# The fourteenth image's store cut into 112 partitions and four pieces of four

## The chip, the cores and the metric

The kernel runs on one core of a Trainium2 chip. Its time is the device time of one execution in microseconds (us), and the median over several executions is what is compared. One execution was also taken with the hardware profiler. A core has sixteen DMA engines that carry all loads and stores, and five instruction streams: PE (TensorE), DVE (VectorE), ACT (ScalarE), POOL (GpSimd) and SP (SyncE), the last of which only issues transfers here.

## The reference

The kernel computes a 3 x 3 convolution with dilation 2 and zero padding, over 16 images of 64 channels and 64 x 64 pixels, to 128 output channels, in float32.

```python
batch, c_in, h, w, c_out, k, dilation = 16, 64, 64, 64, 128, 3, 2
...
x_pad = np.pad(x, ((0, 0), (0, 0), (pad, pad), (pad, pad)), mode='constant')
...
output[b, co] += weight[co, ci, kh, kw] * x_pad[b, ci, kh*dilation:kh*dilation+h, kw*dilation:kw*dilation+w]
```

The output of one image is 128 channels of 64 x 64 float32 values, 16 KB a channel and 2 MB in all; sixteen images are 33.55 MB. The input is half of that.

## The kernel before

Two images are worked on at a time, since one has 64 input channels and there are 128 partitions. The loop over `pb` (line 174 on) runs over the eight pairs; `hb` is 0 or 1 for the two images of a pair, so image number `2 * pb + hb`, counted from 0. The fourteenth image is number 13: `pb` is 6 (`NP - 2`) and `hb` is 1.

A pair's input is loaded by POOL's queue (`load`, line 72), which turns float32 into float16 on the way. POOL then adds pairs of rows (`prepare`, line 127); with these sums the kernel gets two output rows out of fewer products (`phase`, line 171, on PE). ACT copies the part that two outputs share out of PSUM (line 192), and DVE adds it to each of the two other parts and writes the finished rows into an output tile `o` (line 198). An output tile has one channel in each of the 128 partitions, with 16 KB in each.

The stores stand at the end of the loop over `u`, the four quarters of an image. All of them are issued by SP, in program order, on one queue (line 209). The first and the last pair leave in two halves of 1 MB for each image (8 KB in each partition), and all others in one transfer of 2 MB (16 KB in each partition). So there are 20 stores in all: 4 + 12 + 4. The fourteenth image's is the last of the 2 MB ones; after it come the four 1 MB halves of images 14 and 15.

The kernel's own order is kept (`manual_schedule`), and the framework adds the semaphores. Each transfer reports to a semaphore on landing; SP's transfers take eight such semaphores in turn, the load of the weights (line 63) being the first. Ahead of a transfer that takes a semaphore again, the framework puts an instruction on SP that waits until the earlier transfer with that semaphore, eight before it, has landed. At the end of the program (line 240) SP waits for all transfers.

Of the kernel before, what the change touches and what calls it, by code (L numbers as in the profile page):

```python
# [10 lines left out]
def kernel(  # L11
# [7 lines left out]
    nc = tc.nc  # L19
# [7 lines left out]
    P = 128  # L27
    f32 = mybir.dt.float32
    f16 = mybir.dt.float16
    NP = B // 2  # L30
# [38 lines left out]
    def load(pb, cuts):  # L69
        x16[pb] = x16pool.tile([P, H, W], f16, tag="x16", name=f"x16_{pb}")  # L70
        for lo, hi in zip(cuts, cuts[1:]):
            nc.gpsimd.dma_start(out=x16[pb][:, lo:hi], in_=x_pair[pb, :, lo:hi])  # L72
# [21 lines left out]
    for name, a in (("w21", 2), ("w01", 0)):  # L94
        for u in range(2):
            nc.vector.tensor_sub(  # L96
                out=w16[:, SLOT[name] * KW : (SLOT[name] + 1) * KW, u, :],
# [5 lines left out]
    for n, name in enumerate(("w1", "w21", "w0", "w01", "w2")):  # L103
        ps = cpool.tile([P, NB], f32, tag="ps", name=f"wt{n}")
        k0 = SLOT[name] * KW
        for j in range(KW):
            nc.tensor.matmul(  # L107
                out=ps[:, j * CO : (j + 1) * CO],
# [12 lines left out]
    def prepare(pb, lo, hi):  # L121
        if pb not in s16:
            s16[pb] = sumpool.tile([P, 2 * NQ, W], f16, tag="s16", name=f"s16_{pb}")
        src = x16[pb].rearrange("p (q e r) w -> p q e (r w)", e=2, r=2)
        dst = s16[pb].rearrange("p (q r) w -> p q (r w)", r=2)
        q0, q1 = lo // 4, hi // 4
        nc.gpsimd.tensor_add(  # L127
            out=dst[:, q0:q1], in0=src[:, q0:q1, 0, :], in1=src[:, q0:q1, 1, :]
        )
# [37 lines left out]
    def phase(pb, u, terms):  # L167
        ps = [cpool.tile([CO, NB], f32, tag="ps", name=f"ps{hb}") for hb in range(2)]
        for pair in zip(*(conv(pb, hb, ps[hb], u, terms) for hb in range(2))):
            for m in pair:  # L170
                nc.tensor.matmul(**m)  # L171
        return ps

    for pb in range(NP):
        o = [
            opool.tile([P, H, W], f32, tag="o", name=f"o{pb}_{hb}") for hb in range(2)
        ]
        ov = [t.rearrange("p (q e r) w -> p q e (r w)", e=2, r=2) for t in o]
        for u in range(NU):

            if u == 1 and AHEAD <= pb + 2 < NP:
                load(pb + 2, [0, H])
            if pb + 1 < NP:
                if u == 1:
                    prepare(pb + 1, 0, 36)
                elif u == 2:
                    prepare(pb + 1, 36, H)

            s32 = []
            for hb, ps in enumerate(phase(pb, u, [("w1", 2, 0)])):  # L190
                s = spool.tile([P, NB], f32, tag="s32", name=f"s32_{hb}")
                nc.scalar.copy(out=s, in_=ps)  # L192
                s32.append(s)
            for e, terms in enumerate(
                ([("w21", 1, 0), ("w0", 1, -1)], [("w01", 0, 0), ("w2", 0, 1)])
            ):
                for hb, ps in enumerate(phase(pb, u, terms)):
                    nc.vector.tensor_add(  # L198
                        out=ov[hb][:, u * UQ : (u + 1) * UQ, e, :],
                        in0=ps.rearrange("p (q c) -> p q c", c=QW),  # L200
                        in1=s32[hb].rearrange("p (q c) -> p q c", c=QW),
                    )


            step = NU // 2 if pb in (0, NP - 1) else NU
            if (u + 1) % step == 0:
                fl = slice((u + 1 - step) * 4 * UQ, (u + 1) * 4 * UQ)
                for hb in range(2):
                    nc.sync.dma_start(out=out[2 * pb + hb, :, fl], in_=o[hb][:, fl])


# [33 lines left out]
```

## Time and profile before

| What | Value |
|---|---|
| Median of 3 executions | 128.56 us (127.48 to 129.21) |
| The profiled execution's own time | 128.92 us |
| Its span, first to last instruction | 127.1 us |
| PE busy | 105.3 us (83%) |
| DVE busy | 83.2 us (65%) |
| ACT, POOL busy | 38.8 us, 39.6 us |
| Stores, queue 1 | 3024 packets, 33.85 MB with the weights, 63.1% of 16 engines |
| Loads, queue 0 | 1296 packets, 8.39 MB as written, 32.5% of 16 engines |
| Mean rate of DMA over the span | 333 GB/s |

The difference between the profiled time and its span, 1.8 us, lies outside of the first and the last instruction. A packet here is one row of a transfer: the part that lies in one partition, 16 KB or 8 KB in the stores. Besides these there are 4-byte packets, with which each engine reports that its part of a transfer is done; sixteen such reports make a landing. The trace has the time of each packet and of each report, though not the number of the engine.

### The profile page before, as it was taken

The page shows a single profiled execution, that of the slowest core. Times are in us where ns is not written, and L with a number is a line of the kernel's source. Part 1 is how long each engine was busy: PE and PEld are TensorE (multiplying, and loading weights), DVE is VectorE, ACT ScalarE, POOL GpSimd, SP SyncE. Part 2 cuts the span into 40 slices and gives each one's busy share as a digit, 9 for nine tenths or more (in the row PEclk, how much of TensorE's full clock was granted, in tenths as well). Part 3 has the DMA queues.
Part 4 walks back from the last instruction along what each step waited for, and adds up shares of the span by engine and source line. Part 5 has one row for each costly group of instructions (what it writes and reads, how often), then busy time and mean ns, then how long its engine had stood idle before and what let it go on. Part 6 is the DMA issues. An engine that isn't in the chain of part 4 may idle for free.

```text
span 127.1 us, 2415 instructions
## 1 busy us (share of the span) xinstructions
PE 105.3 (83%) x981; PEld 53.4 (42%) x981; DVE 83.2 (65%) x136; ACT 38.8 (31%) x69; POOL 39.6 (31%) x33
## 2 busy tenths in 40 slices
PE   6329999999999999999999999999999999900000
PEld 2014455555555555555555555555555555400000
DVE  0540577787778777877777787778777877740000
ACT  4723033333333333333333333333333333300000
POOL 6039798668094019302900390000000000000000
PEclk9975699999999999999999999999999999985555
DMA  4899999999999999999999999999999999999940
GB/s 107 152 206 226 214 214 216 250 294 281 402 302 265 312 317 325 399 376 309 304 389 428 423 423 438 433 423 423 433 428 433 418 428 433 433 399 430 430 204 13
DMA packets 4330, 42.38 MB, mean 333 GB/s; under 512 B 480, under 2 KB 480, under 8 KB 864
## 3 DMA queue, kind: packets, MB, share of 16 engines
q1 hardware_dynamic: 3024, 33.85, 63.1%
q0 software_dynamic: 1296, 8.39, 32.5%
q8 instruction: 7, 0.11, 0.3%
q14 instruction: 3, 0.02, 0.0%
HBM read 17.07 MB, written 33.55 MB: 398 GB/s over the span
## 4 chain that ended last, share of the span: by engine, by line
PE 79%; DMA 6%; POOL 1%; issue 1%; DVE 1%; DVEq 0%; POOLq 0%
PE ps L171 79%; DMA x<-in_x_dram 6%; POOL s L127 1%; DVE o L198 1%; DVEq L240 0%; POOLq L226 0%; DVEq L198 0%
## 5 line engine op out<-in xcount | busy, mean ns | idle before, releaser
L198 DVE TENSOR_TENSOR o<-ps,s 128x512 f32<-128x512 f32 x128 | 79.7, 684 | 25.1 <-PE ps L171 22.6
L171 PE MATMUL ps<-x,w_sb 64*128 64x496 f16 (+3 forms) x768 | 86.0, 370 | 0.0
L171 PEld LDWEIGHTS <-w_sb 64*128 64x128 f16 x960 | 51.9, 95 | 52.2 <-issue 4.9
L192 ACT COPY s<-ps 128x512 f32<-128x512 f32 x64 | 34.4, 589 | 68.2 <-issue 60.8
L127 POOL TENSOR_TENSOR s<-x 128x1152 f16<-128x1152 f16 (+4 forms) x18 | 34.0, 1912 | 35.5 <-PE ps L171 29.2
L171 PE MATMUL ps<-s,w_sb 64*128 64x496 f16 (+1 forms) x192 | 26.4, 379 | 2.7 <-POOL s L127 2.7
L72 POOL DMA_DIRECT2D x<-in_x_dram x9 | 5.1, 570 | 0.8 <-POOLq L226 0.8
L87 PE MATMUL warm<-zero 128*128 128x512 f16 x6 | 2.7, 630 | 1.2 <-DVE zero L81 1.2
L96 DVE TENSOR_TENSOR w<-w 128x192 f16<-128x192 f32 x4 | 1.7, 494 | 2.5 <-DMA w<-in_weight_dram 2.5
L93 ACT CAST w<-w 128x576 f16<-128x576 f32 x2 | 2.3, 1217 | 1.6 <-DMA w<-in_weight_dram 1.6
L107 PE MATMUL wt<-ident,w 128*128 128x128 f16 x15 | 1.0, 220 | 2.1 <-ACT w L93 2.1
L116 DVE CAST w_sb<-wt 128x384 f16<-128x384 f32 x3 | 1.5, 550 | 1.0 <-PE wt L107 1.0
L107 PEld LDWEIGHTS <-w 128*128 128x128 f16 x15 | 0.8, 98 | 3.0 <-ACT w L93 3.0
L87 PEld LDWEIGHTS <-zero 128*128 128x128 f16 x6 | 0.7, 138 | 2.3 <-DVE zero L81 1.2
L93 ACT ACT_TABLE_LOAD x1 | 1.3, 1283 | 0.7 <-PEq L226 0.7
L118 ACT CAST w_sb<-wt 128x384 f16<-128x384 f32 x2 | 0.9, 482 | 0.6 <-PE wt L107 0.6
L81 DVE MEMSET zero<- 128x256 uint32 x1 | 0.3, 272 | 0.9 <-PEq L226 0.9
masks.py:199 POOL TENSOR_SCALAR_AFFINE_SELECT ident<-ident 128x128 f16<-128x128 f16 x1 | 0.3, 292 | 0.1
masks.py:197 POOL MEMSET ident<- 128x128 f16 x1 | 0.2, 231 | 0.0
L226 POOL MEMSET const-float32-0.0<- 128x1 f32 x1 | 0.1, 98 | 0.2 <-issue 0.2
L226 POOL MEMSET const-bfloat16-1.0<- 128x1 bf16 x1 | 0.1, 101 | 0.0
L226 POOL MEMSET const-uint8-127<- 128x1 uint8 x1 | 0.1, 101 | 0.0
(1 smaller groups left out, 0.1 us busy)
## 6 DMA issues: line engine op xcount, KB each, us to landing
out_dram<-o SPq DMA_DIRECT2D x12, 2048.0 KB, 17.9
out_dram<-o SPq DMA_DIRECT2D x8, 1024.0 KB, 14.0
x<-in_x_dram POOLq DMA_DIRECT2D x7, 1024.0 KB, 15.0
x<-in_x_dram POOLq DMA_DIRECT2D x1, 576.0 KB, 7.1
x<-in_x_dram POOLq DMA_DIRECT2D x1, 448.0 KB, 8.5
w<-in_weight_dram SPq DMA_DIRECT2D x1, 288.0 KB, 2.9
```

What stands on the lines that cost most here:

```text
L72: nc.gpsimd.dma_start(out=x16[pb][:, lo:hi], in_=x_pair[pb, :, lo:hi])
L87: nc.tensor.matmul(out=warm, lhsT=zero[:, 0:P], rhs=zero, start=True, stop=True)
L93: nc.scalar.copy(out=w16[:, 0:NK, u, :], in_=w32k)
L96: nc.vector.tensor_sub(out=w16[:, SLOT[name] * KW : (SLOT[name] + 1) * KW, u, :], in0=w32k[:, a * KW : (a + 1) * KW, :], in1=w32k[:, KW : ...
L107: nc.tensor.matmul(out=ps[:, j * CO : (j + 1) * CO], lhsT=w16[:, k0 + j, :, :].rearrange("o t i -> o (t i)"), rhs=ident, start=True, stop= ...
L116: nc.vector.tensor_copy(out=dst, in_=ps[:, 0 : KW * CO])
L118: nc.scalar.copy(out=dst, in_=ps[:, 0 : KW * CO])
L127: nc.gpsimd.tensor_add(out=dst[:, q0:q1], in0=src[:, q0:q1, 0, :], in1=src[:, q0:q1, 1, :])
L171: nc.tensor.matmul(**m)
L192: nc.scalar.copy(out=s, in_=ps)
L198: nc.vector.tensor_add(out=ov[hb][:, u * UQ : (u + 1) * UQ, e, :], in0=ps.rearrange("p (q c) -> p q c", c=QW), in1=s32[hb].rearrange("p (q ...
L226: nc = _bacc.Bacc("TRN2", target_bir_lowering=False, num_devices=1)
```

## The change

One store of the twenty, that of the fourteenth image, becomes five: partitions 0 to 111 in one transfer, and then 112 to 115, 116 to 119, 120 to 123 and 124 to 127, each in one of its own. The same 2 MB go from the same tile to the same place. All other stores are as they were, and so is everything else.

```diff
                 for hb in range(2):
-                    nc.sync.dma_start(out=out[2 * pb + hb, :, fl], in_=o[hb][:, fl])
+
+                    parts = [0, P]
+                    if (pb, hb) == (NP - 2, 1):
+                        parts = [0, *range(P - 16, P + 1, 4)]
+                    for lo, hi in zip(parts, parts[1:]):
+                        nc.sync.dma_start(
+                            out=out[2 * pb + hb, lo:hi, fl], in_=o[hb][lo:hi, fl]
+                        )
```

## The prediction

> **What bounds the kernel now.** I began with the slices of the span. The first three lines below are the PE row, the DMA row and the rate, 3.18 us a slice.
>
> ```profile
> PE   6329999999999999999999999999999999900000
> DMA  4899999999999999999999999999999999999940
> GB/s 107 152 206 226 214 214 216 250 294 281 402 302 265 312 317 325 399 376 309 304 389 428 423 423 438 433 423 423 433 428 433 418 428 433 433 399 430 430 204 13
> ```
>
> PE is done after slice 35, at about 111 us. The DMA engines are full from slice 3 to 38, and once the loads are over (slice 22 on) they stand at 418 to 438 GB/s, a ceiling that nothing crosses for long. The last two slices are the oddity: 204 and 13 GB/s. Next, the chain of work that ended last: its last pieces are DVE's and it stops at 112.77 us, 14 us ahead of the end of the span. What follows is in SP's waits.
>
> ```profile
> 110.89 0.68 DVE o L198
> ...
> 112.17 0.60 DVE o L198
> ```
>
> ```profile
> SPq L240 <- DMA out_dram<-o: 12.0, 5, 2.4
> SPq L209 <- DVE o L198: 4.8, 2, 4.7
> ```
>
> Five waits of some 2.4 us each: SP stands at the program's end and sees the last five stores land one after another. The end is set by landings, not by arithmetic. Then the tail by windows (window, length, five engines' busy time, clock, DMA share, GB/s), and the DMA view of the last stretch, 123.3 to 127 us.
>
> ```profile
> 120.00:121.00 1.00, 0.00 (x0) 0.00 (x0) 0.00 (x0) 0.00 (x0) 0.00 (x0) 0.50 1.01 426
> 121.00:122.00 1.00, 0.00 (x0) 0.00 (x0) 0.00 (x0) 0.00 (x0) 0.00 (x0) 0.50 0.81 344
> 122.50:123.00 0.50, 0.00 (x0) 0.00 (x0) 0.00 (x0) 0.00 (x0) 0.00 (x0) 0.50 0.24 98
> 124.00:125.00 1.00, 0.00 (x0) 0.00 (x0) 0.00 (x0) 0.00 (x0) 0.00 (x0) 0.50 0.06 25
> ```
>
> ```profile
> DMA packets 8, 0.06 MB, mean 15 GB/s; under 512 B 1, under 2 KB 1, under 8 KB 1
> q1 hardware_dynamic: 8, 0.06, 3.7%
> ```
>
> A share of 0.06 is one engine of sixteen. Fifteen engines have finished by 123.3 us; one works on alone at 25 GB/s through seven rows of 8 KB and its report. The trace's reports of the last store come at 121.40 us (first), 123.56 (fifteenth) and 126.07 (sixteenth). So the kernel ends 2.5 us late because of one laggard. Its lag grew through the run (0.36 us at the store that landed at 75.2 us, 2.16 at 106.2, 2.54 at 116.3): its 16 KB rows mostly took 634 to 661 ns where the others' took 611, until PE stopped.
>
> **The change part by part.** One row of 16 KB occupies an engine for 0.607 us (a 611 ns packet, the next one starting 4 ns before its end; 16 x 16,384 B / 0.607 us is 432 GB/s, the ceiling above). A store of 128 rows is 8 rows an engine, 4.86 us.
>
> Removed: the fourteenth image's transfer loses 16 rows. If 112 rows are dealt evenly, each engine has 7, one less: -0.61 us on every engine, the laggard too.
>
> Added: four transfers of four rows. The trace has no transfer of fewer than 128 rows, so this is bounded. Lower end: the rows go to four engines, the same four each time, at full speed and not to the laggard. These four get 7 + 4 = 11 rows, +1.82 us, and end at 123.56 + 1.82 = 125.38 at the latest; the laggard ends at 126.07 - 0.61 = 125.46. Sum: -0.61 us. Upper end: the four rows of a piece leave as through one engine, because they sit on one or share one way out of the memory. A piece then takes 4 x 0.607 = 2.43 us, four take 9.71, and with the 7 rows before them (4.25) that is 13.96 against 4.86, +9.10 us. The engines concerned would have reported between 121.40 and 123.56, so they report between 130.50 and 132.66: +4.43 to +6.59 us on the end, in the middle +5.5. Between the two, I take the upper. The row of the trace that is nearest to a small transfer is the lone stretch above, the only place where fewer than sixteen engines carry rows, and there rows move at 25 GB/s, one after another. The lower end needs three things at once (four engines, no sharing, the laggard not among them); the upper needs one. It is a choice without a direct row for it, and both ends stay.
>
> [...]
>
> The 112 rows: seven rows an engine don't sit as eight did. If two engines share a way for all of it, seven rows cost up to 4.25 us more, if not, nothing. No row shows it; I take nothing in the middle, since the streams at the ceiling lose nothing to each other, and half of it, 2.1 us, for the top of the range.
>
> Instructions on SP: four more issues of 0.33 to 1.02 us (the rows of this line), each with a 0.22 us semaphore wait ahead of it. The five issues begin at 100.42 us and by the dear price end at 100.42 + 5 x 1.24 = 106.6, where the next store is issued at 105.86 now: up to 0.8 us late. Cost nothing, as the engines have rows of the fourteenth image until the first report of it at 111.61. Without that backlog it would be 0.8.
>
> Waits moved: eight semaphores in turn. The small pieces wait for images 6 to 9, all landed by 95.89 us. Images 14 and 15, first halves, now wait for images 10 and 11 (101.04 and 106.20; issued at 105.86 and 106.46), image 14's second half for image 12 (111.36; issued at 112.19): nothing. The last store, issued at 112.79 now, waits for the 112 rows, which land at 116.30 - 0.61 = 115.7. It is issued at 115.9, and its first packet follows 1.0 us (the weights: issue 0.74, packet 1.74) to 3.7 us later (the first store: 19.27, 22.99), at 116.9 to 119.6. The earliest engine wants it at about 118 (it reports the store before at 118.96), the laggard at 123. Early engines may idle up to 1.6 us and would still report by 119.6 + 2.45 + 0.4 = 122.5, under the end; only the program's end is queued behind it on SP. Cost nothing; without the laggard's cover up to 1.6.
>
> Sum against the profiled 128.92 us: -0.61 removed, the rest in the +9.10 on the four engines, less the 2.5 to 4.7 us that they finish early: +5.5, so 134.4 us in such an execution. The median of runs lies 0.36 below it: 134.1.
>
> **The rivals.** *It balances.* The lower end is the truth: the laggard gives up one row, four others take three each, and all end near 125.4. Time 128.56 - 0.61 = 127.95, faster and not slower. For it: the lag is real (2.5 us), and -0.61 and +1.82 meet almost exactly. Against it: the three conditions. It turns into the forecast where a small row takes long enough: slower by 2% (2.57 us) begins when the four engines report at 128.64, 5.08 us or 8.4 rows later than the fifteenth does now, that is when the four small rows take 9.4 row times, 1.43 us each.
>
> *The laggard is among the four,* or rows share in part: 126.07 + 1.82 = 127.89, time 130.4, inside of 2%. For it: nothing tells which engine lags; against: four of sixteen.
>
> *It does less or more than it says.* If a row goes to the engine that carried it in the 128-row store, whichever transfer it is in, loads are as before: 128.56. If 112 rows keep their engines and the laggard loses four, it gains at most 4 x 0.607 = 2.43 us, and the time is 126.1 at best, still under 2%. For these: nothing but the constant order of the reports from store to store.
>
> **How the numbers follow.** Forecast (small pieces go as through one engine) 0.56; it balances 0.22; laggard among them or part sharing 0.14; less or more than it says 0.08. The likeliest gives 134.1; its own range is 128.56 + 4.43 = 133.0 less a us for partly staggered engines, 132.0, to 128.56 + 6.59 + 2.1 = 137.3. For 8 in 10 the whole must hold the balanced case with the scatter of the runs (0.7 us): 127.3 to 137.3. A change of 2% is about what a measurement of this kernel can tell from none. Slower than that: 0.58, the forecast and a tail of part sharing; within: 0.37; faster: 0.05, the best of the third rival with a favourable scatter.
>
> **What would show it.** If right: the windows show a share of about 0.25 or less, near 27 to 110 GB/s, for some 5 us at the end, instead of 0.06 for 2.5; 16 KB packets after about 110 us last 1.2 to 2.4 us instead of 611 ns; the fourteenth image's small issues land 2.4 us apart. If it balances: packets stay at 611 ns, five engines end together near 125.4, and the lone stretch is gone. The last issue near 115.9 us instead of 112.8 would show the semaphore step right. A median under 131.1 us makes the forecast wrong, and packets that stay at 611 ns make its reason wrong.

## The result, and the profile after

The changed kernel took 133.89 us (median of 6, 131.90 to 137.08) against 128.47 us before: a ratio of 1.033, interval 1.027 to 1.040. Repeated on two more occasions beside other kernels it was 1.047 (1.041 to 1.054) and 1.036 (1.031 to 1.042). Ratios leave out executions more than 1.5% above the fastest of their kernel, so that the medians of the changed kernel, which scatters widely, lie further from those before than its ratios say, and of the profiles of such executions (the two halves and the 112 rows alone, further down, among them) only packets, rates and landings are read. The profile shown here is of an execution of the second occasion, at 132.86 us with a span of 131.1.

The slices of the changed kernel (3.28 us each; PE, DMA, rate):

```profile
PE   6339999999999999999999999999999999000000
DMA  4899999999999999999999999999999999999720
GB/s 105 151 222 211 227 212 197 285 280 307 410 312 285 330 307 320 350 315 320 355 425 440 420 425 440 420 430 435 425 435 410 430 437 352 330 345 400 315 97 15
```

PE ends at 111 us as before. The new thing is in the rate: slices 34 to 37 (from 108 us) hold 352, 330, 345 and 400 GB/s where 399 to 433 stood, and in the same slices the DMA row still says 9. The engines are busy all the time and move about a sixth less (357 GB/s in the mean of the four against 424). This is the sign to look for: a busy share that doesn't fall while the rate does. The same in one stretch, before and then after (window, length, busy times, clock, DMA share, GB/s):

```profile
112.00:116.00 4.00, 0.00 (x0) 0.00 (x0) 0.77 (x2) 0.00 (x0) 0.00 (x0) 0.70 0.99 420
```

```profile
112.00:116.00 4.00, 0.00 (x0) 0.00 (x0) 0.41 (x1) 0.00 (x0) 0.00 (x0) 0.90 0.97 326
```

Share 0.99 and 420 GB/s became 0.97 and 326, a good fifth less. In the packet records, of the packets with 16 KB that start from 105 to 121 us, one of 195 was over 700 ns before (956 ns, beside a fetch of instructions); after, 44 of 197 are, up to 2.66 us: five at 1.27 us, twice the usual 0.611, three near 1.9, three times, and the rest spread between 0.7 and 2.66. Together the 44 last 26 us longer than at 611 ns.

The tail:

```profile
121.00:122.00 1.00, 0.00 (x0) 0.00 (x0) 0.00 (x0) 0.00 (x0) 0.00 (x0) 0.50 1.01 426
122.50:123.00 0.50, 0.00 (x0) 0.00 (x0) 0.00 (x0) 0.00 (x0) 0.00 (x0) 0.50 0.89 377
124.00:125.00 1.00, 0.00 (x0) 0.00 (x0) 0.00 (x0) 0.00 (x0) 0.00 (x0) 0.50 0.47 197
126.00:127.00 1.00, 0.00 (x0) 0.00 (x0) 0.00 (x0) 0.00 (x0) 0.00 (x0) 0.50 0.18 74
128.00:129.00 1.00, 0.00 (x0) 0.00 (x0) 0.00 (x0) 0.00 (x0) 0.00 (x0) 0.50 0.06 25
```

Instead of one engine alone (share 0.06) from 123.3 to 125.6 us, the engines now drop out one after another until 129.4. The last store's reports run from 122.25 to 129.77 us; before, from 121.40 to 126.07. SP's waits changed their form:

```profile
SPq L247 <- DMA out_dram<-o: 12.6, 1, 12.6
SPq L214 <- DMA out_dram<-o: 8.1, 2, 4.4
```

Five waits at the end became one, since the first thing that SP waits for there is now the last store: it shares its semaphore with the 112 rows. The second line holds two waits at the stores. The longer, 4.4 us, is the new one, for the 112 rows: they landed at 116.75 us and the last store was issued at 116.81. The other ends with the landing of the thirteenth image at 111.91. The new wait cost nothing: the first engine reported the store before at 119.82 and the last store at 122.25, 2.43 us later, so its rows followed without a gap.

### The profile page after: what moved, and what is told of

Same layout as the page of the kernel before. It is cut to its first block, busy times and chain, and to the rows that moved or that the text cites. A ratio compares the mean times of both kernels' runs of the same rounds, so it can differ in the third digit from the quotient of the medians.

```text
span 132.4 us, 2419 instructions
## 1 busy us (share of the span) xinstructions
PE 106.3 (80%) x981; PEld 54.7 (41%) x981; DVE 83.3 (63%) x136; ACT 38.9 (29%) x69; POOL 39.6 (30%) x33
## 4 chain that ended last, share of the span: by engine, by line
PE 76%; DMA 4%; POOL 1%; issue 1%; DVE 1%; DVEq 0%; POOLq 0%
PE ps L171 76%; DMA x<-in_x_dram 4%; POOL s L127 1%; DVE o L198 1%; DVEq L247 0%; POOLq L233 0%; DVEq L198 0%
## 5 line engine op out<-in xcount | busy, mean ns | idle before, releaser
L107 PE MATMUL wt<-ident,w 128*128 128x128 f16 x15 | 1.8, 312 | 2.1 <-ACT w L93 2.1
L107 PEld LDWEIGHTS <-w 128*128 128x128 f16 x15 | 1.5, 145 | 3.0 <-ACT w L93 3.0
```

The lines of the kernel that those rows point to most:

```text
L107: nc.tensor.matmul(out=ps[:, j * CO : (j + 1) * CO], lhsT=w16[:, k0 + j, :, :].rearrange("o t i -> o (t i)"), rhs=ident, start=True, stop= ...
```

## The experiments

Three theories went into the runs, each a guess that the two profiles left open. *Shared way*: neighbouring partitions share one way out of the memory, and engines that come to it together wait for each other. *Imbalance*: four engines carry eleven rows. *Transfer count*: five transfers, their reports and the later last issue cost something by themselves. Each edit below stands in place of the store of the fourteenth image alone; in the first five kernels it is cut down to the list of the pieces, by partitions and columns of the tile, each of which is a transfer of its own.

**Five transfers, cut along the columns** (c1_columns).

```diff
+ [(slice(0, P), slice(a, b)) for a, b in ((0, 56), (56, 58), (58, 60), (60, 62), (62, 64))]
```

> The fourteenth image leaves in five transfers again, with the same bytes in each (56 and four times 2 of the 64 image rows of every channel), but each from all 128 partitions. Shared way (four neighbouring partitions have one way out of the memory, so a piece of four goes at one engine's rate): nothing is shared anew, so it runs like the kernel before, ratio 1.00 within 0.01, packets of 14 KB and 512 B at their usual rate. Imbalance (four engines carry eleven rows): every engine has the same bytes, 1.00 as well. Transfer count (five transfers, their reports, and the last issue that now waits for the first of the five to land): like the changed kernel, 1.03. This run separates the third theory from the other two.

Measured: 1.006 (1.002 to 1.010). Transfer count is out as the main cause: about a sixth of the change's cost, and little over a third by the unfavourable ends of both intervals (1.010 and 1.027). No 16 KB packet was over 700 ns there and no 14 KB packet over 576. In the same stretch:

```profile
112.00:116.00 4.00, 0.08 (x2) 0.00 (x0) 1.55 (x3) 0.00 (x0) 0.00 (x0) 0.85 1.01 404
```

Share and rate stay together, but for 512 B packets, which mostly take 27 ns where 512 B at the rate of a 16 KB row would take 19. Of the 0.7 us that the ratio says, these explain 0.26 (32 packets an engine, 8 ns each); the rest, within the interval, stays open.

**Two halves** (c3_halves).

```diff
+ [(slice(0, 64), fl), (slice(64, P), fl)]
```

> The fourteenth image leaves as partitions 0 to 63 and 64 to 127: two transfers, and if 64 rows are dealt to sixteen engines as four each, every engine still has eight rows. Shared way, if it is a fixed group of partitions that has one way at 27 GB/s and the lower 64 have half of the ways: sixteen engines crowd on half of the ways, some 16 KB packets take about 1.2 us, and the image takes up to twice its 4.86 us: later by 1.5 to 4.9 us, ratio 1.01 to 1.04. Imbalance: all engines have equal rows, 1.00. Transfer count: one transfer more, 1.00 to 1.01.

Measured: 1.036 (1.031 to 1.040), as much as the change, with two transfers and no piece of four anywhere. Of its 16 KB packets from 105 to 121 us 71 were over 700 ns, and 31 lay between 1.18 and 1.30 us. The first half landed from 110.38 to 112.38 us, the second from 113.35 to 120.84.

```profile
112.00:116.00 4.00, 0.00 (x0) 0.00 (x0) 1.07 (x2) 0.00 (x0) 0.00 (x0) 0.98 0.90 227
```

A share of 0.90 at 227 GB/s: sixteen engines move little more than eight would at a row in 0.607 us (27.0 GB/s each, 216 in all). Each half has sixteen reports, so that every engine has its eight rows if the rows are dealt evenly. Such a split costs as much as the whole change, and imbalance isn't needed for it. The 27 GB/s of the expectation are this rate of one engine; that a way has a rate of its own, and which partitions have it in common, was a guess that the run doesn't show.

**The 112 rows alone** (c5_only112, repeated as c5b_only112 in five rounds).

```diff
+ [(slice(0, P - 16), fl)]
```

> The fourteenth image's first 112 partitions leave in one transfer and the last 16 are left out (their output is not written). What it costs alone: if seven rows an engine disturb nothing, every engine has one row less and the last landing comes 0.61 us earlier, ratio 0.995; if two engines share a way for a good part of it, packets of 1.2 us and up to 3.6 us later, ratio up to 1.03. Shared way with the pieces as the main cost: 0.99 to 1.01, so that most of the change's 1.033 lies in the four pieces. Imbalance: 0.995. Transfer count: 0.995.

> The 112 rows alone again, the last 16 rows of the fourteenth image left out, for the split on one chip: 1.015 to 1.025 if it is as before. The changed kernel less this is what the four pieces add: 1 to 3%.

Measured: 1.020 (1.018 to 1.022) and 1.017 (1.012 to 1.023). I had expected 0.99 to 1.01 here, and this is the miss that matters: an eighth of the work of one store fewer, and yet 2.2 to 2.5 us slower. About half of the harm that I had put on the small pieces comes with the big one (1.7 to 2.0% of 3.3 to 3.6%). In the stretch, the share stays and the rate falls as in the changed kernel:

```profile
112.00:116.00 4.00, 0.00 (x0) 0.00 (x0) 1.20 (x2) 0.00 (x0) 0.00 (x0) 0.99 0.99 356
```

That engines with seven rows each no longer keep to ways of their own is the reading that fits. It is argued and not shown: the trace doesn't say which engine reads which partition, and no run tried 112 rows in another order.

**Strided pieces** (c2_strided, repeated as c2b_strided in five rounds).

```diff
+ [(slice(0, P - 16), fl)] + [(slice(P - 16 + j, P, 4), fl) for j in range(4)]
```

> The first 112 partitions in one transfer and four pieces of four partitions, as in the change, but a piece takes every fourth partition (112, 116, 120, 124, and so on) rather than four neighbours. Same number of transfers, same rows, four reports a piece, eleven rows on four engines. Shared way: the four rows of a piece have four different ways, so the pieces' packets fall back from 0.9 to 2.6 us to near 0.61 us (up to 1.2 where an engine meets the way's usual user), and of the 5.0 us that the last landing came later some 3 to 5 us go: ratio to before 1.00 to 1.015. Imbalance: no difference to the change, 1.03. Transfer count: no difference, 1.03.

> 112 partitions and four strided pieces again; its profile had the last piece landed at 118.1 us against 121.3 in the changed kernel, but its ratio was no better, on another chip. Shared way: on one chip it lies below the changed kernel by 0.5 to 2% and above the 112 rows alone. If the pieces' neighbourhood does not matter beside the 112 rows: the same as the changed kernel within 0.5%.

Measured first 1.034 (1.028 to 1.040), as if the neighbourhood of the four rows didn't matter, and against the expectation. On one chip with the changed kernel, though, 1.027 (1.023 to 1.032) against 1.036 (1.031 to 1.042): strided pieces cost less by 0.9%, or 1.1 us. This is likely and no more, since the two intervals overlap a little and the same strided kernel moved by 0.7% from one occasion to the other. The first expectation of 1.00 to 1.015 failed, and the 112 rows, which are in this kernel too, cost 1.7 to 2.0% by themselves. In the stretch the strided kernel is no faster than the changed one (326 GB/s), so that this view doesn't tell the two apart:

```profile
112.00:116.00 4.00, 0.27 (x4) 0.00 (x0) 1.73 (x3) 0.00 (x0) 0.00 (x0) 0.87 0.95 295
```

**Sixteen rows in one transfer** (c4_one16).

```diff
+ [(slice(0, P - 16), fl), (slice(P - 16, P), fl)]
```

> The 16 rows leave as one transfer of 16 partitions instead of four of four, so that, if sixteen engines take one row each, every engine has its eight rows again and no imbalance is left. Shared way: the 112 rows stay out of step with the ways, and the 16 neighbouring rows crowd on four of them: 1.015 to 1.035, 16 KB packets of 1.2 us and more. Imbalance: 1.00.

Measured: 1.022 (1.015 to 1.029), where the 112 rows alone are 1.017 on the same chip. With even rows on the engines again (sixteen reports for the sixteen rows) more than half of the change's 1.036 is still there. The sixteen neighbouring rows add 0.5% to the 112 rows alone, within the intervals, so that the crowding on them that I had expected isn't seen apart from the loss of the 112.

**Pieces alone, as extra work behind an untouched store** (c6_neighbours, c7_strided, c8_far).

```diff
                     nc.sync.dma_start(out=out[2 * pb + hb, :, fl], in_=o[hb][:, fl])
+                    if (pb, hb) == (NP - 2, 1):
+                        for j in range(4):
+                            nc.sync.dma_start(
+                                out=extra[4 * j : 4 * j + 4], in_=o[hb][4 * j : 4 * j + 4]
+                            )
```

The second has `o[hb][j:16:4]` there, the third `o[hb][112 + 4 * j : 112 + 4 * j + 4]`; `extra` is a tensor in device memory that nobody reads.

> The kernel before, whose fourteenth image leaves from all 128 partitions at once, and right behind it four extra transfers of four rows each, which go to a scratch tensor in device memory: partitions 0 to 3, 4 to 7, 8 to 11, 12 to 15. So four engines carry 12 rows of 16 KB instead of 8, and nothing else changes sides. Shared way (four neighbouring partitions have one): a piece goes at one engine's rate where the four engines come to it together, 4 x 0.607 = 2.4 us, 9.7 us for all; less where they come one after the other, since a leading engine passes freely (in the changed kernel one of the four did, at 0.6 us a piece). Fully together the four engines report 131.1 to 133.3 us instead of 121.4 to 123.6; I expect 3 to 6 us later than before, ratio 1.02 to 1.05, packets of 1.2 to 2.4 us. Imbalance alone: 4 x 0.607 = 2.43 us more on engines that have 2.5 us to spare: 1.00 to 1.005.

> As the run with neighbouring rows, with the same four extra transfers into the same places of the same scratch tensor, but a piece takes partitions j, j + 4, j + 8 and j + 12. Only the partitions that are read differ. Shared way: four different ways, in the 128-row store those of the same four engines, so the packets stay at 0.61 us and only the imbalance is left, 2.43 us against 2.5 us of slack: ratio 1.00 to 1.005. If what is shared lies on the side of the device memory, or is a price of short transfers: the same as the run with neighbouring rows.

> As the run with neighbouring rows, but the extra pieces read partitions 112 to 115, 116 to 119, 120 to 123 and 124 to 127, the ones of the change. Shared way: the four engines crowd as with partitions 0 to 15, and here the ways belong to other engines, which are slowed too: 1.03 to 1.06, not less than the run with partitions 0 to 15. Imbalance: 1.00 to 1.005.

Measured: neighbours 1.031 (1.024 to 1.037), strided 1.011 (1.008 to 1.014), far neighbours 1.061 (1.054 to 1.068). The three write the same number of bytes to the same places in the same number of transfers; they differ in the partitions that they read, and in nothing else. The stretch, neighbours, then strided, then far:

```profile
112.00:116.00 4.00, 0.00 (x0) 0.00 (x0) 0.47 (x1) 0.00 (x0) 0.00 (x0) 1.00 0.96 360
```

```profile
112.00:116.00 4.00, 0.00 (x0) 0.00 (x0) 1.05 (x2) 0.00 (x0) 0.00 (x0) 0.73 0.98 416
```

```profile
112.00:116.00 4.00, 0.04 (x1) 0.00 (x0) 1.33 (x3) 0.00 (x0) 0.00 (x0) 1.00 0.99 334
```

The strided pieces leave no trace in the packets: one of 216 over 700 ns, again a single one of 956. A piece's four reports come 0.6 us after those of the piece before (one engine's: 112.44, 113.08, 113.67, 114.30), one row time each. With neighbours the same four pieces landed at 113.77, 114.77, 116.94 and 119.01, and eight packets were over 1.1 us, up to 2.2; far, they landed at 116.01, 119.27, 121.58 and 123.44, with packets up to 3.8 us. That other engines are at work on those partitions would explain this; the trace doesn't name the engines. So what is shared lies on the side of the partitions, not of the device memory. What is left with strided pieces, 1.011, fits the imbalance, four rows more on four engines, together with some part for the four transfers more; no run takes these two apart.

**The changed kernel beside its parts** (a1_after, a2_after), no edit.

> The changed kernel again, on the same chip as the pieces alone, so that the parts can be set beside the whole: 1.033 as before. Shared way: with 1.020 for the 112 rows alone and 2 to 5% for four pieces that are extra, the whole is less than the sum of its parts, since the pieces here replace rows and the queues wait for the last of both only once.

> The changed kernel once more, beside three of its parts on one chip, in five rounds. 1.033 and 1.047 so far on two chips; I expect 1.03 to 1.05. Shared way: more than either part alone. Imbalance: the same as every kernel with the same rows on the same engines, the strided pieces among them.

Measured: 1.047 and 1.036, given above. In the second set, on one chip: 112 rows alone 1.017, with strided pieces 1.027, with neighbours 1.036. No version came out ahead of the kernel before. Moving rows off a late engine in some other way was not tried.

## Why the prediction was right, and where its terms were not

The time (134.1 us predicted, 133.89 measured), the sign and the kind of cause were right. The sum reached its size through terms that were mis-sized in opposite directions, so that a miss of 0.2 us is luck. By the ratios the change costs 4.3, 6.1 and 4.6 us on its three occasions, where 5.5 was forecast.

*What bounds the kernel*: right. The end is set by landings. In each of the fourteen profiles the last report of all follows the last report of the fourteenth image, or of the extra pieces behind it, by 9.7 to 9.8 us: the slowest engine then has four halves to go, eight rows of 8 KB and 2.44 us each. So whatever delays the slowest engine at that image delays the end by as much.

*The 112 rows*: the term that failed. The prediction took 0 of a possible 4.25 us, "since the streams at the ceiling lose nothing to each other". That holds for the 128-row stores here (one packet of 195 over 700 ns) and says nothing of another grouping. Measured, the 112 rows alone are 0.017 x 127.69 = 2.2 us slower though each engine has a row less, if the rows are dealt evenly, so regrouping costs about 2.2 + 0.61 = 2.8 us, an estimate that takes the row saved at its full price. The stretched packets are in good part its own: those over 700 ns lose 17.6 and 22.6 us in the two profiles of the 112 rows alone, against the 26 us of the changed kernel.

*The four pieces*: right in kind, too dear. I had taken 2.4 us a piece, all four engines together, +9.10 us on each and 5.5 on the end over all. In the changed kernel the last report of the pieces came at 115.76, 117.49, 118.78 and 119.97 us, 1.2 to 1.7 apart (1.6 to 2.6 in its two other profiles), where the prediction's sign was 2.4. The first of the four engines got through at 113.09, 114.05, 114.70 and 115.83. That is 0.65 to 1.13 apart, nearer to one row time: a leading engine passes more freely and the others come later. In this profile the pieces did set the end: the fourth one's last report came 9.80 us ahead of the end, and the 112 rows, complete at 116.75, would have allowed an end 3.2 us earlier. By the ratios, the pieces are worth 1.036 - 1.017 = 1.9%, 2.5 us on the end: some 0.9% for being neighbours and 1.0% for the rest, eleven rows on four engines among it, each with an uncertainty nearly as large. Alone, without regrouped rows to stand behind, four neighbouring pieces from the same partitions cost 1.061 - 1.011 = 5.0%, 6.4 us, more than the forecast's middle, and landed 1.9 to 3.3 us apart (what is taken off here is the run with strided pieces from partitions 0 to 15). The parts don't add up; that late engines wait once for both is a guess.

The split was thus some 2.2 + 2.5 = 4.7 us in that set, against 5.5 forecast from the pieces alone.

*SP's issues and waits*: right. The four small issues were over by 104.24 us, ahead of the next store at 105.51, and the last issue slid to 116.81, as the step said (115.9), with no gap behind it.

*The laggard*: here the prediction, and its rival *It balances*, leaned on one execution. The lag of the last engine behind the fifteenth at the twelfth image's landing, ahead of anything that was changed, was 2.17 us in the profile before; in the thirteen other profiles of this study it was 0.04 to 2.87 with a median of 0.51. So the 2.5 us of slack, which made +1.82 look free and -0.61 look like a gain, were that execution's. The strided extra pieces, predicted to fit into the slack (1.00 to 1.005), cost 1.011 for that reason or another; their profile had a lag of 0.37.

*The rivals*: balance fell, since rows stretch (44 of 197 over 700 ns). That a row stays with its engine whichever transfer it is in fell by its time, 128.56 us against 133.89 measured; each small piece had four reports, but the trace doesn't say from which engines. That the laggard is one of the four is refuted for the two profiles where pieces meet a lag of over 2 us at the thirteenth image (3.18 and 2.49). With neighbouring extra rows the last engine reported the fourteenth image at 116.66 us, when all four had reported the first piece already (113.77). In the changed kernel the last engine reported the thirteenth image at 111.91; seven rows later, if the 112 are dealt evenly, it is 116.2, and the first piece was complete at 115.76.

*The two ends of the term for the pieces*: both fit the runs in part, together. The lower end had four engines for a piece: each small piece has one update of its semaphore at its issue and four later, where the 112 rows have sixteen. The upper end had four rows leave as through one engine: in the profile shown here the pieces' last reports came 1.2 to 1.7 us apart, between one row time (0.607) and four (2.43), and the halves ran at 227 GB/s, in a stretch that already held some rows of the next store, against 420 before. Setting the two against each other was the mistake; one says how many engines come, the other what they find. Which partitions share a way, if that is the cause, no run shows. What the engines find was an open question for the 112 rows too, from the start.

## What to carry to other kernels

With all DMA engines busy (a share of 0.90 to 0.99 from 112 to 116 us), a store's shape was part of its rate here: transfers from all 128 partitions ran nearly without stretched packets (one of 195 over 700 ns), while the 112 rows alone lost 17.6 and 22.6 us in packets over 700 ns, and of the halves' packets 71 were over 700 ns, 31 of them at about twice the usual length, though each half had sixteen reports, and the 112 rows have them in the changed kernel. Look for a DMA share that stays near 1 while GB/s fall (0.97 at 326 here), and at packets of two and three times the usual length; then ask which partitions meet, before counting rows for each engine. And take slack from several profiles, not from one.

## What the runs showed of the hardware that was not expected

A 2 MB store cut into halves of 64 partitions delayed the end by 3.6%, 4.5 us, nearly the whole time of the image again (4.86 us). Small pieces that read partitions 112 to 127 were twice as harmful as those from 0 to 15 (6.1% against 3.1%). And an engine's lag of up to 2.9 us comes and goes between executions of the same stores; what causes it was not tried.
